# A hybrid decoder layer: the last residual addition leaves the vector engines and is done by accumulating stores

## The chip, the cores and the metric

The kernel runs on one core of a Trainium2 chip. The core has five engines that work side by side and meet through semaphores: TensorE (PE, with its weight loads shown as PEld), VectorE (DVE), ScalarE (ACT), GpSimd (POOL) and SyncE (SP). Sixteen DMA engines move data between the device memory (HBM) and the on-chip memory (SBUF). SP, ACT and POOL issue transfers; those of SP and ACT run on hardware queues, those of POOL on a software queue.

The metric is the device time of one execution in microseconds (us). It was 1841.93 us as the median of three runs (1841.57 to 1843.07).

## The reference

One inference step of a one-layer decoder trunk on 256 prompt tokens and 8 x 8 sample tokens, 320 tokens in all, with a model width of 2048. Cut to what bears on the change:

```python
def decoder_layer(x, ssm_state, ssm_conv_state, ffn_conv_state, p):
    h = rms_norm(x, p["norm_mix_pre"])
    proj = h @ p["w_in"]
    ...
    mix = jnp.concatenate([gate_out, ssm_out], axis=-1) @ p["w_out"]
    x = x + rms_norm(mix, p["norm_mix_post"])
    f, new_ffn_conv = conv_ffn(rms_norm(x, p["norm_ffn_pre"]), ffn_conv_state,
                               p["ffn_w_up"], p["ffn_conv_w"], p["ffn_conv_b"], p["ffn_w_down"])
    x = x + rms_norm(f, p["norm_ffn_post"])
    return x, new_ssm, new_ssm_conv, new_ffn_conv, chunk_v
```

The second-last `x` is called x1 in the kernel. The output y is x1 plus the normed FFN result f, and this last line is the one that the change rewrites. The norm is f times the reciprocal root of the mean of its squares over the width (one number for each token), times a weight for each column.

## The kernel before

Activations lie transposed: 128 partitions carry the columns of one of 16 column blocks (KD = 16), and the free dimension carries the 320 tokens (NT = 320). A tile such as `acc` is therefore 128 x 16 x 320 in single precision. The output `o_y` in HBM has the same layout, so that a store of two column blocks writes 128 rows of 2 x 320 numbers, 2560 bytes each.

Every matmul is done as three on TensorE: weights and activations are each split into a high and a low part, and high x high, high x low and low x high are summed (lines 128 to 130, in `accumulate`). Weights stream in as slabs of 512 KB (`slab`): SP loads a slab into one of three raw buffers (line 115), ScalarE makes the high part (line 117, three buffers), VectorE the low part (line 119, three buffers). The raw buffer is free for the next load once VectorE has read it.

The kernel runs in two halves. The first, the mixers, ends with x1 in `acc_mix` (line 962). The second, the FFN, has eleven groups g of 512 columns each. `ffn_up(g)` multiplies by the up-projection, applies the short convolution and the gate; `chunk_out(ffn_w_down, g, ...)` multiplies by the down-projection and adds the result to `acc_ffn` (line 210, VectorE). The loop runs one group ahead: `ffn_up(g + 1)` stands in the program before `chunk_out` of group g. Instructions are put in order by a list scheduler that goes by program order and by when they are ready.

In the last group `last(nb)` follows each column block: ScalarE squares it (line 258), GpSimd or, for the last two blocks, VectorE adds the squares up (line 259), and ScalarE multiplies the block by the norm's weight (line 1065). After the last block comes the tail. TensorE sums the squares over the columns (`token_sums`, line 241), VectorE forms the reciprocal root in eleven small operations (`rsqrt_of`, lines 224 to 230), and TensorE spreads it to all partitions (`spread`, line 248), where it stays in PSUM as `r4`. Then, for q from 0 to 7, two column blocks at a time:

```python
        for q in range(KD // n):
            ks = slice(n * q, n * q + n)
            f = acc[:, ks, :]
            dve.tensor_tensor(out=f, in0=f, in1=r4.unsqueeze(1).to_broadcast([P, n, NT]), op=ALU.mult)
            (dve if q in (2, 5, 7) else pool).tensor_tensor(out=f, in0=f, in1=x1[:, ks, :], op=ALU.add)
            (sp, act)[q % 2].dma_start(o_y[:, ks, :], f)
```

The multiplication is line 1084, the addition line 1085 (three on VectorE, five on GpSimd), the store line 1086 (four from SP, four from ACT). `o_y` isn't written anywhere else.

Of the kernel before, what the change touches and what calls it, by code (L numbers as in the profile page):

```python
# [9 lines left out]
F32 = mybir.dt.float32  # L10
# [3 lines left out]
ALU = mybir.AluOpType  # L14
# [3 lines left out]
P = 128  # L18
# [3 lines left out]
NT = NP + NS  # L22
D = 2048
KD = D // P
# [10 lines left out]
def hybrid_step(  # L35
# [10 lines left out]
    act, dve, pool, pe, sp = nc.scalar, nc.vector, nc.gpsimd, nc.tensor, nc.sync  # L46
# [10 lines left out]
    def misc(name):  # L57
        return ms.tile([P, 512], F32, tag="ms", name=name)
# [45 lines left out]
    def first():  # L104

        return tc.high_priority(offset=200000)
# [3 lines left out]
    def slab(src):  # L110
        n = src.shape[2]
        with tc.high_priority(offset=100000):
            m = n * src.shape[1]
            raw = wp.tile([P, 1024], F32, tag="wraw", name="wraw", bufs=3)
            slab_load.append(sp.dma_start(raw[:, :m].rearrange("p (a n) -> p a n", n=n), src).ins)
            hi = wp.tile([P, 1024], F32R, tag="whi", name="whi", bufs=3)
            act.copy(hi[:, :m], raw[:, :m])  # L117
            lo = wp.tile([P, 1024], F32R, tag="wlo", name="wlo", bufs=3)
            dve.tensor_tensor(out=lo[:, :m], in0=raw[:, :m], in1=hi[:, :m].bitcast(F32), op=ALU.subtract)  # L119

        def block(k, c):
            o = k * n + c * P
            return hi[:, o:o + P], lo[:, o:o + P]
        return block

    def accumulate(ps, w, xhi, xlo, first, last):
        whi, wlo = w
        pe.matmul(ps, whi, xhi, start=first, stop=False)  # L128
        pe.matmul(ps, whi, xlo, start=False, stop=False)  # L129
        return pe.matmul(ps, wlo, xhi, start=False, stop=last).ins  # L130

    def rows_of(w, k0, nk, c0, n):
        return w[k0 * P:(k0 + nk) * P, c0:c0 + n].rearrange("(k p) n -> p k n", p=P)
# [6 lines left out]
    def tick():  # L140
        while bg:
            try:
                next(bg[0])
                return
            except StopIteration:
                bg.pop(0)
# [51 lines left out]
    def chunk_out(w, ck, hi, lo, begins, done=None, rate=1):  # L198

        for nb in range(KD):  # L200
            if nb % 2 == 0:
                wb = slab(rows_of(w, 4 * ck, 4, P * nb, 256))
            ps = mm.tile([P, 512], F32, tag="mm", name=f"pd_{ck}_{nb}")
            for k in range(4):
                made = accumulate(ps[:, :NT], wb(k, nb % 2), hi[:, k, :], lo[:, k, :], k == 0, k == 3)
            with first():
                if begins:
                    act.copy(acc[:, nb, :], ps[:, :NT])
                else:
                    dve.tensor_tensor(out=acc[:, nb, :], in0=acc[:, nb, :], in1=ps[:, :NT], op=ALU.add)  # L210
            if done is not None:
                done(nb)
            if nb % 2 == 1:
                for _ in range(rate):
                    tick()
        pd_last.append(made)


    def rsqrt_of(ss, scale, n, rows=P):

        v = tp.tile([P, n], F32, tag=f"rs_v{n}", name="rs_v")[:rows]
        r = tp.tile([P, n], F32, tag=f"rs_r{n}", name="rs_r", bufs=3)[:rows]
        t = tp.tile([P, n], F32, tag=f"rs_t{n}", name="rs_t")[:rows]
        dve.tensor_scalar(out=v, in0=ss, scalar1=scale, scalar2=EPS, op0=ALU.mult, op1=ALU.add)
        dve.tensor_scalar(out=r.bitcast(I32), in0=v.bitcast(I32), scalar1=-0.5, scalar2=float(0x5F3759DF),
                          op0=ALU.mult, op1=ALU.add)
        for _ in range(3):
            dve.scalar_tensor_tensor(out=t, in0=v, scalar=-0.5, in1=r, op0=ALU.mult, op1=ALU.mult)
            dve.tensor_tensor(out=t, in0=t, in1=r, op=ALU.mult)
            ins = dve.scalar_tensor_tensor(out=r, in0=t, scalar=1.5, in1=r, op0=ALU.add, op1=ALU.mult).ins  # L230
        rsqrt_ins.append(ins)
        return r
# [3 lines left out]
    def token_sums(*sqs):  # L236

        ps = misc("tsum")
        for c, o in enumerate((0, P, NT - P)):
            for i, sq in enumerate(sqs):  # L240
                pe.matmul(ps[:, c:c + 1], sq[:, o:o + P], ones[:, 0:1], start=i == 0, stop=i == len(sqs) - 1)
        return ps[:, 0:3]

    def spread(r, out=None):

        ps = misc("spread")
        for c, o in ((2, NT - P), (0, 0), (1, P)):
            pe.transpose(ps[:, o:o + P], r[:, c:c + 1].to_broadcast([P, P]), ident)
        if out is not None:
            act.copy(out, ps[:, :NT])  # L250
        return ps[:, :NT]
# [69 lines left out]
    with ExitStack() as mctx:  # L321
        op = mctx.enter_context(tc.tile_pool(name="op", bufs=1))
# [305 lines left out]
        with tc.tile_pool(name="sd", bufs=1) as sd:  # L628
# [307 lines left out]
            with first():  # L936
# [4 lines left out]
                r = rsqrt_of(ps, 1.0 / D, 3)  # L941
# [35 lines left out]
    x1 = acc  # L977


    with tc.tile_pool(name="fp", bufs=1) as fp:  # L980
# [88 lines left out]
        for g in range(NG):  # L1069
            hi, lo = nxt  # L1070
            if g < NG - 1:
                nxt = ffn_up(g + 1)
            if g == 0:
                acc = fp.tile([P, KD, NT], F32, name="acc_ffn")
            chunk_out(ffn_w_down, g, hi, lo, g == 0, last if g == NG - 1 else None)

        act.dma_start(o_fconv_p, ptf)

        r4 = spread(rsqrt_of(token_sums(sq4), 1.0 / D, 3))
        n = 2  # L1080
        for q in range(KD // n):
            ks = slice(n * q, n * q + n)
            f = acc[:, ks, :]
            dve.tensor_tensor(out=f, in0=f, in1=r4.unsqueeze(1).to_broadcast([P, n, NT]), op=ALU.mult)
            (dve if q in (2, 5, 7) else pool).tensor_tensor(out=f, in0=f, in1=x1[:, ks, :], op=ALU.add)
            (sp, act)[q % 2].dma_start(o_y[:, ks, :], f)


_OUTS = [
# [81 lines left out]
```

## Time and profile before

| | |
|---|---|
| median of three runs | 1841.93 us |
| the profiled execution | 1841.51 us |
| its span, first to last instruction | 1839.8 us |
| mean granted TensorE clock | 0.988 |
| last matmul of the FFN starts | 1820.16 us |
| factor spread over the partitions, ends | 1825.95 us |
| last VectorE addition ends | 1836.23 us |
| data moved by DMA | 294.65 MB, of it 14.82 MB written to HBM |

How to read the rows: L1084 is line 1084 of the kernel. A row of groups gives the line, the engine, the operation, output<-input, and the shortest, median and longest duration in nanoseconds, then the first and last start in us. A row of the timeline or of the chain of waits begins with the start and the duration in us; in brackets stands how long the engine sat idle before, and what ended it. A "q" behind an engine's name means its queue of transfers. A row of queues gives packets, megabytes and the share of sixteen engines' time. "DMA to landing" is the time from the issue to the arrival of the last byte. A row of DMA tenths or GB/s cuts its window into 40 equal slices. A row of windows begins with the stretch in us; then come its sum, the busy time and count of PE, PEld, DVE, ACT and POOL, the granted clock, the DMA share and GB/s.

### The profile page before, as it was taken

The numbers are of one execution on the slowest core, as the hardware profiler recorded it, in microseconds if no ns is written. First come the engines' busy times: TensorE is split into PE (matmuls) and PEld (weight loads), VectorE is DVE, ScalarE is ACT, GpSimd is POOL, SyncE is SP. The second block draws the span as 40 slices with busy tenths as digits, with TensorE's granted clock in tenths as the row PEclk, the third lists the DMA queues.
The fourth block names the chain that finished last, engine by engine and source line by source line (L and its number), as shares of the span: only waits on it lengthen the run. The fifth ranks groups of instructions, "written<-read, shape, count | busy, mean of one in ns | idle before, by whom it ended". The sixth has DMA issues, their size and how long they took to land.

```text
span 1839.8 us, 31095 instructions
## 1 busy us (share of the span) xinstructions
PE 1790.7 (97%) x12185; PEld 1749.9 (95%) x12185; DVE 1188.5 (65%) x2050; ACT 786.2 (43%) x1077; POOL 305.2 (17%) x624
## 2 busy tenths in 40 slices
PE   8999999999999999999899999999999999999996
PEld 8999999999888889999799999999999999999995
DVE  4448854556986968676876475656465665756575
ACT  5442544334434545344454443333334343434334
POOL 1001210000331321103522020101011010201004
PEclk8999999999999999999899999999999999999998
DMA  8655654445566465555455545554545555455542
GB/s 265 178 141 172 167 149 148 149 147 158 178 184 207 138 205 159 170 161 188 152 163 156 153 150 151 155 152 150 152 150 152 150 152 150 153 150 155 153 154 92
DMA packets 222994, 294.65 MB, mean 160 GB/s; under 512 B 16736, under 2 KB 150464, under 8 KB 222656
## 3 DMA queue, kind: packets, MB, share of 16 engines
q1 hardware_dynamic: 210256, 269.72, 48.8%
q10 hardware_dynamic: 10448, 16.10, 2.4%
q0 software_dynamic: 2144, 6.85, 1.3%
q8 instruction: 96, 1.57, 0.4%
q14 instruction: 50, 0.41, 0.1%
HBM read 277.80 MB, written 14.82 MB: 159 GB/s over the span
## 4 chain that ended last, share of the span: by engine, by line
PE 82%; issue 6%; DVE 5%; DMA 4%; POOL 1%; ACT 1%; ACTq 0%; POOLq 0%; DVEq 0%; SPq 0%
PE ps L128 17%; PE ps L130 17%; PE ps L129 17%; PE pd L129 9%; PE pd L128 9%; PE pd L130 9%; DVE wlo L119 1%; DMA out_ssm_state_sample<-st 1%; PE y_ps L830 1%; DMA cs<-dacs_d 1%; DMA st<-in_state_ssm 1%; DMA wraw<-in_w_in 1%; POOL acc_mix L962 1%; PE yo_ps L737 1%; DMA lb<-in_gate_ln_b 1%
## 5 line engine op out<-in xcount | busy, mean ns | idle before, releaser
L119 DVE TENSOR_TENSOR wlo<-wraw,whi 128x1024 fp32r<-128x1024 f32 (+1 forms) x476 | 588.1, 1236 | 444.4 <-ACT whi L117 442.5
L117 ACT CAST whi<-wraw 128x1024 fp32r<-128x1024 f32 (+1 forms) x476 | 496.9, 1044 | 763.2 <-PE ps L129 446.1
L128 PE MATMUL ps<-h_hi,whi 128*128 128x320 f32 x2528 | 787.9, 312 | 10.0 <-ACT whi L117 5.3
L130 PE MATMUL ps<-h_hi,wlo 128*128 128x320 f32 x2528 | 784.4, 310 | 2.0 <-DVE wlo L119 2.0
L129 PE MATMUL ps<-h_lo,whi 128*128 128x320 f32 x2528 | 783.9, 310 | 0.0
L128 PEld LDWEIGHTS ps<-h_hi,whi 128*128 128x128 f32 x2528 | 477.2, 189 | 15.3 <-ACT whi L117 6.4
L130 PEld LDWEIGHTS ps<-h_hi,wlo 128*128 128x128 f32 x2528 | 477.0, 189 | 4.3 <-DVE wlo L119 3.3
L129 PEld LDWEIGHTS ps<-h_lo,whi 128*128 128x128 f32 x2528 | 477.1, 189 | 1.4 <-issue 0.9
L128 PE MATMUL pd<-fhi,whi 128*128 128x320 f32 x704 | 217.5, 309 | 0.0
L129 PE MATMUL pd<-flo,whi 128*128 128x320 f32 x704 | 217.5, 309 | 0.0
L130 PE MATMUL pd<-fhi,wlo 128*128 128x320 f32 x704 | 217.5, 309 | 0.0
L128 PE MATMUL pd<-ohi,whi 128*128 128x320 f32 x448 | 140.4, 313 | 0.0
L129 PE MATMUL pd<-olo,whi 128*128 128x320 f32 x448 | 139.1, 311 | 0.0
L130 PE MATMUL pd<-ohi,wlo 128*128 128x320 f32 x448 | 138.7, 310 | 0.0
L128 PEld LDWEIGHTS pd<-fhi,whi 128*128 128x128 f32 x704 | 132.2, 188 | 0.0
L129 PEld LDWEIGHTS pd<-flo,whi 128*128 128x128 f32 x704 | 132.2, 188 | 0.0
L130 PEld LDWEIGHTS pd<-fhi,wlo 128*128 128x128 f32 x704 | 132.2, 188 | 0.0
L1016 POOL COPY ptf<-pad 128x2 f32<-128x2 f32 x88 | 21.1, 240 | 597.8 <-DVE pad L1004 597.3
L210 DVE TENSOR_TENSOR acc_ffn<-acc_ffn,pd 128x320 f32<-128x320 f32 x160 | 77.5, 484 | 39.5 <-PE pd L130 38.0
L128 PEld LDWEIGHTS pd<-ohi,whi 128*128 128x128 f32 x448 | 84.1, 188 | 2.8 <-issue 2.2
L129 PEld LDWEIGHTS pd<-olo,whi 128*128 128x128 f32 x448 | 84.1, 188 | 1.6 <-issue 1.2
L130 PEld LDWEIGHTS pd<-ohi,wlo 128*128 128x128 f32 x448 | 84.1, 188 | 0.2 <-issue 0.2
(271 smaller groups left out, 1594.8 us busy)
## 6 DMA issues: line engine op xcount, KB each, us to landing
wraw<-in_ffn_w_up SPq DMA_DIRECT2D x176, 512.0 KB, 3.7
wraw<-in_w_in SPq DMA_DIRECT2D x144, 512.0 KB, 3.7
wraw<-in_ffn_w_down SPq DMA_DIRECT2D x88, 512.0 KB, 3.5
wraw<-in_w_out SPq DMA_DIRECT2D x64, 512.0 KB, 3.5
st<-in_state_ssm SPq DMA_DIRECT2D x40, 256.0 KB, 3.5
out_ssm_state_sample<-st ACTq DMA_DIRECT2D x32, 256.0 KB, 2.7
cs<-dacs_d SPq DMA_DIRECT2D x16, 320.0 KB, 4.2
xr<-in_xT SPq DMA_DIRECT2D x4, 640.0 KB, 4.3
```

Of the source, the lines that this page charges most:

```text
L117: act.copy(hi[:, :m], raw[:, :m])
L119: dve.tensor_tensor(out=lo[:, :m], in0=raw[:, :m], in1=hi[:, :m].bitcast(F32), op=ALU.subtract)
L128: pe.matmul(ps, whi, xhi, start=first, stop=False)
L129: pe.matmul(ps, whi, xlo, start=False, stop=False)
L130: return pe.matmul(ps, wlo, xhi, start=False, stop=last).ins
L210: dve.tensor_tensor(out=acc[:, nb, :], in0=acc[:, nb, :], in1=ps[:, :NT], op=ALU.add)
L737: pe.matmul(ps_yo[row:row + 32, :256], cms[:, b, :], st[:, 256 * r:256 * r + 256], start=b % 4 == 0, stop=b % 4 == 3, tile_position=(0, row))
L830: pe.matmul(ps[64 * i:64 * i + 64, cols], w(hl), x(hl, m, cpx), tile_position=(0, 64 * i), **flags)
L962: added.append((dve if kt < 2 else pool).tensor_tensor(out=a, in0=a, in1=xr[q][:, k, :], op=ALU.add).ins)
L1016: pool.tensor_copy(ptf[:, k, :], pad[:, 256:258])
```

## The change

x1 is stored to the output `o_y` whole, by one transfer on ACT's queue, at the second FFN group (g = 1), ahead of that group's `chunk_out`. In the tail the additions of x1 are gone. Each multiplied pair of column blocks is stored by GpSimd's queue with an accumulating transfer, which adds it to what `o_y` holds. The pair q = 7 comes first in the program and is multiplied by GpSimd. Since GpSimd reads its factor from SBUF, ScalarE copies `r4` from PSUM into a new tile `r4s`. The other seven pairs are multiplied by VectorE as before, in the order 0 to 6.

```diff
             if g == 0:
                 acc = fp.tile([P, KD, NT], F32, name="acc_ffn")
+            if g == 1:
+                act.dma_start(o_y, x1)
             chunk_out(ffn_w_down, g, hi, lo, g == 0, last if g == NG - 1 else None)
 
         act.dma_start(o_fconv_p, ptf)
 
+
         r4 = spread(rsqrt_of(token_sums(sq4), 1.0 / D, 3))
+        r4s = fp.tile([P, NT], F32, name="r4s")
+        act.copy(r4s, r4)
         n = 2
-        for q in range(KD // n):
+
+        for q in (KD // n - 1, *range(KD // n - 1)):
             ks = slice(n * q, n * q + n)
             f = acc[:, ks, :]
-            dve.tensor_tensor(out=f, in0=f, in1=r4.unsqueeze(1).to_broadcast([P, n, NT]), op=ALU.mult)
-            (dve if q in (2, 5, 7) else pool).tensor_tensor(out=f, in0=f, in1=x1[:, ks, :], op=ALU.add)
-            (sp, act)[q % 2].dma_start(o_y[:, ks, :], f)
+            on, r = (pool, r4s) if q == KD // n - 1 else (dve, r4)
+            on.tensor_tensor(out=f, in0=f, in1=r.unsqueeze(1).to_broadcast([P, n, NT]), op=ALU.mult)
+            pool.dma_start(o_y[:, ks, :], f, accum_op=ALU.add)
```

## The prediction

> **What bounds the kernel now.** I read the busy shares first, then the chain of waits over the last 24 us, then each engine's timeline and the DMA traffic after the last matmul.
>
> ```profile
> span 1839.8 us, 31095 instructions
> ...
> PE 1790.7 (97%) x12185; PEld 1749.9 (95%) x12185; DVE 1188.5 (65%) x2050; ACT 786.2 (43%) x1077; POOL 305.2 (17%) x624
> ```
>
> TensorE sets the pace nearly everywhere, and the change removes no matmul. So it can gain only where TensorE stands still, and what it adds earlier costs only if it makes TensorE wait. The standstill is the tail:
>
> ```profile
> 1820.16 0.16 PE pd L130
> ...
> 1825.03 0.92 PE spread L248 x3
> 1825.97 3.01 DVE acc_ffn L1084 x4
> 1828.98 1.60 DVE acc_ffn L1085
> 1830.58 2.19 DVE acc_ffn L1084 x3
> 1832.77 1.38 DVE acc_ffn L1085
> 1834.15 0.74 DVE acc_ffn L1084
> 1834.92 1.31 DVE acc_ffn L1085
> ```
>
> From 1825.97 to 1836.23 the chain is VectorE alone: eight multiplications (one each 0.74 to 0.75 us apart) and three additions; GpSimd's five additions run beside it. This is the stretch that the change attacks. What comes behind VectorE is the last store:
>
> ```profile
> L1086 SPq DMA_DIRECT2D out_y<-acc_ffn x4: 332/344/357, 1828.4 to 1835.6; - x4
> L1086 ACTq DMA_DIRECT2D out_y<-acc_ffn x4: 338/338/338, 1829.9 to 1836.3; - x4
> ...
> DMA to landing us min/median/max: 2.1/2.2/2.2
> ```
>
> The last store is issued at 1836.3 and lands 2.2 later, at 1838.5; 1.3 more pass to the end of the span. Now the traffic of these stores, the window 1826 to 1840 in 40 slices of 0.35 us:
>
> ```profile
> GB/s 0 0 0 0 0 0 0 0 0 227 417 293 0 146 395 432 388 439 73 161 402 373 0 73 432 395 432 388 154 88 424 402 424 402 132 0 0 0 0 0
> ...
> q10 hardware_dynamic: 576, 1.31, 23.5%
> q1 hardware_dynamic: 576, 1.31, 23.5%
> ```
>
> The reader is to see two things. The first slice with traffic is 1829.15 to 1829.5 and about half full, and the first store was issued at 1828.4: 0.7 to 1.0 us pass from an issue to data, and I use 1.0. The last slice with traffic ends at 1838.25, which is 1.55 before the end of the span. And the engines are already busy for 47% of 14 us, which is 6.6 us, at 400 GB/s and more whenever they move: eight stores cost 6.6 us of pure transfer even if they are all ready at once. VectorE's removed work therefore uncovers a transfer floor a few us behind it.
>
> **The change part by part.**
>
> VectorE: three additions go (1.60, 1.38 and 1.31 in the chain) and one multiplication (0.74). Seven are left: 1825.97 + 7 x 0.745 = 1831.2 instead of 1836.23. That is 5.0 us less on the present chain; the question is what ends later.
>
> GpSimd: five additions go. It gets the multiplication of the last two column blocks, ahead of everything else, and it can read the factor only from a copy in SBUF. The nearest rows:
>
> ```profile
> L250 ACT COPY r<-spread x2: 418/418/419, 52.4 to 937.4; 128x320 f32<-128x320 f32 x2
> L1085 POOL TENSOR_TENSOR acc_ffn<-acc_ffn,acc_mix x5: 1526/1542/2124, 1826.9 to 1833.4; 128x640 f32<-128x640 f32 x5
> ```
>
> The copy is the same operation as L250, 0.42 us, and ScalarE is idle there. GpSimd's multiplication has the shape of its additions, 1.54 us; the 2.12 fell to one that ran beside a VectorE addition, which no longer exists. The spread ends at 1825.95; with 0.05 for each of three handovers (the issue gap seen between engines in the chain): copy to 1826.42, multiplication to 1828.02, first accumulating store issued at 1828.07. The other seven stores stand behind this multiplication in GpSimd's queue, so the first of VectorE's results, ready at 1826.7, waits 1.9 us (its store comes second) where today it is handed on at once.
>
> Issue: eight stores leave SP and ACT (0.34 each, no one behind them) and go to GpSimd. Plain loads that GpSimd issues are the only price in the trace:
>
> ```profile
> L580 POOL DMA_DIRECT2D bs<-in_gate_b_s x4: 536/538/567, 56.4 to 404.1; - x4
> ...
> DMA to landing us min/median/max: 4.0/4.1/6.6
> ```
>
> ```profile
> L579 POOL DMA_DIRECT2D w<-in_gate_w x1: 532/532/532, 347.4 to 347.4; - x1
> ...
> DMA to landing us min/median/max: 1.8/1.8/1.8
> ```
>
> An issue takes 0.53 whether it carries 256 KB or 8 KB, so the eighth begins at 1828.07 + 7 x 0.53 = 1831.8, after VectorE's last result at 1831.2: the issues, not VectorE, come last before the transfers. The fixed part of a GpSimd transfer is 1.8 (8 KB, next to no data), that of the present stores 2.2 - 6.6/8 = 1.4. So I add 0.4 to the 1.0 above: data from 1828.07 + 1.4 = 1829.5. Bounds: 0.0 and 1.0 to add.
>
> Transfer: this is the term that no row shows. An accumulating store must fetch the old y beside f, so it moves 2.62 MB more on the read side. **Lower bound**: the second read hides completely, 6.6 us as today. **Upper bound**: each store waits for the one before it; 2.2 + 0.4 for the later start and 0.8 for its second read (6.2 below, over eight) make 3.4, times eight is 27 us. **Taken**: both reads one after the other through the same engines. What reading from HBM costs them at full load is in the traffic of the start, 5 to 25 us, where loads saturate the engines:
>
> ```profile
> DMA  9999999999999799999999999999999999999999
> GB/s 386 416 419 435 410 430 412 367 375 291 264 277 256 295 385 461 406 424 430 389 402 430 410 414 410 406 410 397 307 225 225 217 274 246 234 205 254 352 389 393
> ```
>
> At the 420 GB/s of its better slices 2.62 MB take 6.2 us; 6.6 + 6.2 = 12.8 us. I take it because the present stores leave the engines no spare rate (420 GB/s out, 420 in, each alone). The Trainium skill's page "Collectives: The Full Stack", section "The bandwidth ceiling: the fold count and why AG ≠ RS ≠ AR", says that a reduction in the DMA needs two source reads on the same read ring and measures it at half the rate of a copy (a ratio of 1.93). By that ratio the transfer would be an estimated 12.7 us and the span would end at 1843.75; by the plain store's row it ends at 1837.65. No run so far shows an accumulating transfer.
>
> Store of x1 during the FFN: one issue on ACT, about 0.36 (that of a 1 MB store, below), and 2.62 MB of traffic, 6.2 us at 420 GB/s, among the weight loads. x1 is final after its last addition:
>
> ```profile
> L962 POOL TENSOR_TENSOR acc_mix<-acc_mix,xr x14: 867/1131/1937, 885.7 to 910.3; 128x320 f32<-128x320 f32 x14
> ```
>
> That is before 913 us, and line 1068 to 1075 put the store behind two further up-projections, so nothing behind it on ACT's queue is held for data. Can it delay TensorE?
>
> ```profile
> 1034.06 3.89 SPq L115 DMA_DIRECT2D wraw<-in_ffn_w_up  x2
> ```
>
> ```profile
> 1035.24 1.05 ACT L117 CAST whi<-wraw 128x1024 fp32r<-128x1024 f32 x1 [2.15 <-PE ps L129]
> 1038.76 1.05 ACT L117 CAST whi<-wraw 128x1024 fp32r<-128x1024 f32 x1 [2.47 <-PE ps L129]
> 1042.28 1.05 ACT L117 CAST whi<-wraw 128x1024 fp32r<-128x1024 f32 x1 [2.47 <-PE ps L129]
> ```
>
> ```profile
> L115 SPq DMA_DIRECT2D wraw<-in_ffn_w_up x144: 367/368/379, 1016.6 to 1745.1; - x144
> ...
> DMA to landing us min/median/max: 3.3/3.6/5.1
> ```
>
> With three raw buffers, the load issued at 1034.06 feeds the third cast from there, at 1042.28; it lands after 3.6, so 4.6 us are spare, and behind the cast stand two more slabs of 3.52 us in converted form, less 2.3 for cast and subtraction: 4.7. Together 9.3 against 6.2 of delay if the store went wholly ahead. I cost it at nothing; uncovered, it would be 6.2. An earlier store of 1 MB on ACT's queue speaks for that:
>
> ```profile
> 181.00:187.00 6.00, 6.00 (x43) 6.00 (x42) 6.00 (x12) 2.45 (x3) 1.60 (x2) 1.00 0.90 299
> ```
>
> ```profile
> L565 ACTq DMA_DIRECT2D out_chunk_v_prompt<-vt x1: 362/362/362, 181.0 to 181.0; - x1
> ```
>
> TensorE (the first column behind the sum of 6.00) stays busy for 6.00 of 6.00 us with the engines' share at 0.90. The accumulating stores must wait for this store to land, which is some 800 us earlier.
>
> **Sum.** 1828.07 + 1.4 + 12.8 + 1.55 = 1843.8, against 1839.8: 4.0 us more. The profiled execution took 1841.51, 0.4 under the median of 1841.93; carried to that median the forecast is **1846.0 us**. The break-even is a transfer of 1839.8 - 1.55 - 1829.5 = 8.75 us, 1.33 times the plain one.
>
> **The rivals.**
>
> B, the second read hides. At the tail, read and write sides work at once, the y fetch costs the engines nothing, and each row takes what it takes now. Then 1829.5 + 6.6 + 1.55 = 1837.65: 2.2 less, **1839.8 us**. It decides below 1.33 times the plain transfer. For it: the engines idle in gaps of the present tail, and loads and stores run together at 181 us. Against it: 420 GB/s is reached in either direction alone. Even here the floor is the 6.6 us of bytes: without the added 0.4, 2.6 are gained, not VectorE's 5.0. Only if the scheduler put the first VectorE result's store ahead of GpSimd's multiplication could 1.3 more go.
>
> C, accumulating rows are much dearer, or one store waits for the last. Three times the plain row gives 19.8 us of transfer: 1850.9, 11 more, 1853 us. Wholly serial stores give 1828.07 + 27 + 1.3 = 1856.4, 16.6 more, **1858.5 us**. Against the serial form: today's second store is issued at 1829.9, before the first (1828.4 + 2.2) has landed, so stripes of y aren't held to overlap. For dear rows: nothing in the trace bounds them.
>
> D, the x1 store starves the weight loads: its rows are 20 KB, a load's 1 or 2 KB, and if engines alternate row by row the loads crawl for 6.2 us. The 9.3 us of cover speak against it; uncovered, with the forecast's tail, 1846.0 + 6.2 = **1852 us**. The Trainium skill, "DMA: Bandwidth & Descriptors", section "Queues, rings and completion order", says that an engine alternates between queues by whole packets; that is this rival's mechanism, and the trace above shows it with rows of 8 KB only, without a stall.
>
> E, the change does nothing where it matters: the floor falls at the old end, within 1 us of 1841.9.
>
> **How the numbers follow.** Forecast 0.55, B 0.20, C 0.16, D 0.05, E 0.04. A measurement of this kernel can tell about 0.2%, 3.7 us, from no change. The forecast's own range, from a start of 0.4 earlier or 0.6 later and a transfer of 11 to 14 us, is 1.8 to 5.8 more, 1843.7 to 1847.7; some six tenths of it lie above 3.7. Slower: 0.33 + 0.16 + 0.05 = 0.54. Faster by 3.7 needs B with the other order of GpSimd's queue: 0.04. Within: the rest, 0.42. The range runs from 1839.3, which takes in most of B, to 1853, which takes in D and the milder half of C; about 0.03 lie below it and 0.09 above.
>
> **What would show it.** In the changed profile: seven multiplications on VectorE ending near 1831.2; GpSimd's eight issues at 0.53 from 1828.07 to 1832.3; all traffic of the tail on the software queue, from about 1829.5, dense, and 12.8 us long. If it ends after 6.6 us, the taken price is wrong and B holds; if gaps stand between stores, C. TensorE in the second FFN group should show no new wait on a weight load, and the wraw landing may rise to 10 for two or three loads. The forecast falls if rows of the accumulating queue take under 1.3 times the present ones, or if the tail's start is moved by something upstream.

## The result and the profile after

| | before | after |
|---|---|---|
| median, six runs each | 1842.29 us | 1848.87 us |
| ratio, 95% interval | | 1.0034 [1.0023, 1.0046] |
| once more, 22 and 11 runs | 1841.21 us | 1847.48 us |
| ratio, 95% interval | | 1.0031 [1.0021, 1.0041] |
| span of the profiled execution | 1839.8 us | 1846.0 us |
| "tail": end of the spread to end of the span | 13.85 us | 22.1 us |

The change makes the kernel about 6 us slower; 4 were forecast, with 1.8 to 5.8 as the forecast's own range. I call the stretch from the end of the spread to the end of the span the tail. It is the measure for the profiles, since the work ahead of it starts some microseconds earlier or later from run to run.

First the chain of waits of the changed kernel behind the last matmuls (start, duration, what):

```profile
1823.04 0.92 PE spread L248 x3
...
1823.98 0.43 ACT r4s L1084
1824.41 0.07 issue
1824.48 1.55 POOL acc_ffn L1091
1826.03 0.30 issue
1826.33 6.26 POOL out_y L1092 x7
1832.59 0.89 POOLq L1173
```

VectorE has left the chain. Its own row, from the timeline, ends at 1829.64, 5.7 us after the spread, where it ended 10.3 after it before:

```profile
1824.43 5.21 DVE L1091 TENSOR_TENSOR acc_ffn<-acc_ffn,spread 128x640 f32<-128x640 f32 x7 [1.45 <-ACT r4s L1084]
```

So the change did what it set out to do on VectorE. The stores, by line and by queue (the window of the queue's row is 1826 to 1846):

```profile
L1092 POOL DMA_DIRECT2D out_y<-acc_ffn x8: 937/2092/3304, 1826.3 to 1830.2; - x8
L1076 ACTq DMA_DIRECT2D out_y<-acc_mix x1: 339/339/339, 910.7 to 910.7; - x1
...
DMA to landing us min/median/max: 4.8/9.7/13.7
```

```profile
DMA  0009387998899999999999999999999531000000
GB/s 0 0 0 82 41 113 143 210 169 123 159 179 169 195 200 179 184 210 205 200 215 195 215 195 215 195 220 205 205 210 220 102 61 20 10 0 0 0 0 0
...
q0 software_dynamic: 1152, 2.62, 77.4%
```

Three things are to be seen. The engines are full (nines), yet move some 200 GB/s where the plain stores moved 400 and more. Their busy time is 77.4% of 20 us, 15.5 us, where the plain stores needed 6.6. And the early store of x1 was issued at 910.7, long before the second FFN group: the list scheduler put it right behind x1's last addition, which starts at 908.7.

Finer windows give the ends of that traffic: 1826 to 1834 in slices of 0.2 us, and 1842 to 1846 in slices of 0.1.

```profile
GB/s 0 0 0 0 0 0 0 0 0 205 38 38 90 90 128 102 179 205 205 192 192 166 141 115 115 154 154 166 179 192 192 141 192 192 192 205 192 205 154 192
```

```profile
GB/s 77 51 102 0 77 0 77 0 26 0 26 0 26 0 0 0 0 0 0 0 0 0 0 0 0 0 0 0 0 0 0 0 0 0 0 0 0 0 0 0
```

Traffic begins between 1827.8 and 1828.0 and is thin for 1.2 us behind its first slice; it ends at about 1843.3, after a last 1.3 us in which only a few engines still work. Then 2.7 us pass to the end of the span.

### The profile page after: what moved, and what is told of

It reads as the page before. It is cut to its first block, busy times and chain, and to the rows that moved or that the text cites. A ratio compares the mean times of both kernels' runs of the same rounds, so it can differ in the third digit from the quotient of the medians.

```text
span 1846.0 us, 31083 instructions
## 1 busy us (share of the span) xinstructions
PE 1789.7 (97%) x12185; PEld 1747.7 (95%) x12185; DVE 1183.0 (64%) x2046; ACT 786.8 (43%) x1078; POOL 306.5 (17%) x628
## 4 chain that ended last, share of the span: by engine, by line
PE 84%; issue 6%; DVE 4%; DMA 4%; ACT 1%; POOL 1%; POOLq 0%; SPq 0%; ACTq 0%; DVEq 0%
PE ps L128 17%; PE ps L130 17%; PE ps L129 17%; PE pd L129 9%; PE pd L128 9%; PE pd L130 9%; DVE wlo L119 1%; PE y_ps L830 1%; DMA st<-in_state_ssm 1%; PE yo_ps L737 1%; DMA wraw<-in_w_in 1%; DMA cs<-dacs_d 1%; ACT whi L117 1%; DMA lb<-in_gate_ln_b 1%; PE sg L595 0%
## 5 line engine op out<-in xcount | busy, mean ns | idle before, releaser
L128 PEld LDWEIGHTS ps<-h_hi,whi 128*128 128x128 f32 x2528 | 476.1, 188 | 14.7 <-ACT whi L117 5.7
```

## The experiments

The two theories that had to be told apart first: the price of the tail is the second read of an accumulating store (T1), or the software queue, whose issues took 0.94 us and more instead of 0.53 (T2).

**Plain stores on GpSimd's queue.**

```diff
-            pool.dma_start(o_y[:, ks, :], f, accum_op=ALU.add)
+            pool.dma_start(o_y[:, ks, :], f)
```

> The changed kernel with its eight last stores still on GpSimd's queue but plain: y is f times its norm, x1 is overwritten (the last addition is left out). Theory T1 (the second read is the price): rows fall from 0.239 to 0.10 us, the transfer from 15.5 to about 6.6 us, and the tail from the end of the spread to the end of the span falls from 22.1 to 12.5-14 us; the time is 1.5 us below to 0.5 above the kernel before. Rival T2 (the software queue is slow, because GpSimd writes the descriptors: its issues took 0.9 to 3.3 us instead of 0.53): rows or the gaps between them stay, the transfer stays over 12 us, the tail stays over 19 us and the time 4 us or more above before.

Measured: ratio 0.9981 [0.9971, 0.9991]; span 1836.7, tail 12.9 us. The issues, and the queue's row in the window 1826 to 1836.7:

```profile
L1092 POOL DMA_DIRECT2D out_y<-acc_ffn x8: 539/539/585, 1826.1 to 1829.9; - x8
```

```profile
q0 software_dynamic: 640, 2.62, 61.1%
```

61.1% of 10.7 us is 6.5 us of transfer on the same queue: T1 holds against T2: the price belongs to accumulating and not to the queue. Whether the second read takes the time or the addition itself, no run separates. Even the long issues belong to the accumulation, since the plain ones take 0.54. The queue costs something else, seen in the window 1832.7 to 1836.7 (slices of 0.1 us), beside the kernel free_add below, which stores by SP and ACT, in the window 1830.3 to 1834.3:

```profile
GB/s 410 410 461 410 461 410 461 410 410 410 410 256 154 0 0 0 0 0 0 0 0 0 0 0 0 0 0 0 0 0 0 0 0 0 0 0 0 0 0 0
```

```profile
GB/s 461 410 410 410 410 410 410 410 410 410 410 435 410 410 384 410 435 410 410 410 410 461 256 26 0 0 0 0 0 0 0 0 0 0 0 0 0 0 0 0
```

Thirteen slices with traffic leave 2.7 us to the end of the span, twenty-four leave 1.6. The span ends 1.1 us later behind the software queue, whether the store is plain or accumulates. The other runs agree: 2.7 to 3.0 us where the last stores stand in the software queue, 1.6 to 1.7 where they stand in those of SP and ACT.

**GpSimd's multiplication undone**, and with it the copy of the factor.

```diff
-        for q in (KD // n - 1, *range(KD // n - 1)):
+        for q in range(KD // n):
...
-            on, r = (pool, r4s) if q == KD // n - 1 else (dve, r4)
-            on.tensor_tensor(out=f, in0=f, in1=r.unsqueeze(1).to_broadcast([P, n, NT]), op=ALU.mult)
+            dve.tensor_tensor(out=f, in0=f, in1=r4.unsqueeze(1).to_broadcast([P, n, NT]), op=ALU.mult)
```

> The changed kernel without GpSimd's multiplication: VectorE does all eight, in the order 0 to 7, no copy of the factor. T1 with the transfer as the bound: the first store is issued about 0.8 us after the spread instead of 2.4, so the tail shrinks by 1.5 us, from 22.1 to 20.6, and the time by about 1.5 us (ratio to before about 1.0026 instead of 1.0034). If the issues or VectorE set the end instead: VectorE's last result comes 0.7 us later and the tail is 22 to 23 us.

Measured: ratio 1.0030 [1.0018, 1.0041], tail 21.4 us (spread to 1829.40, span 1850.8). The first store is issued 1.15 us after the spread instead of 2.37, but the tail is only 0.65 shorter. Its traffic begins 2.6 us after the spread instead of 3.9, but the last 1.3 us of it move one row at a time (26 GB/s in every second slice of 0.1 us is a row of 2560 bytes; the window is 1846.8 to 1850.8), where the changed kernel has up to four:

```profile
GB/s 26 0 26 0 26 0 26 0 26 0 26 0 26 0 0 0 0 0 0 0 0 0 0 0 0 0 0 0 0 0 0 0 0 0 0 0 0 0 0 0
```

The difference to the changed kernel's ratio lies inside the intervals; the sign in the profile is as expected, the size under half of the 1.5 us. GpSimd's multiplication shows no gain; VectorE was not last.

**Fewer and larger, more and smaller accumulating stores**, both against dve_all:

```diff
-            pool.dma_start(o_y[:, ks, :], f, accum_op=ALU.add)
+            if q % 2:
+                k4 = slice(n * q - n, n * q + n)
+                pool.dma_start(o_y[:, k4, :], acc[:, k4, :], accum_op=ALU.add)
```

> As dve_all, but the accumulating stores are four of four column blocks each (rows of 5120 bytes) instead of eight of two. If the price goes by bytes (0.239 us per 2560), rows take 0.48, the transfer stays 15.3 us and starts 0.75 us later than in dve_all: tail about 21.3 us. If two reads cost 0.205 and each row or descriptor 0.034 more, rows take 0.445 and the transfer 14.2 us: tail about 20 us. If a cost per store weighs (issue up to 3.3 us), four fewer stores gain more than 2 us.

```diff
-            pool.dma_start(o_y[:, ks, :], f, accum_op=ALU.add)
+            for k in (n * q, n * q + 1):
+                pool.dma_start(o_y[:, k, :], acc[:, k, :], accum_op=ALU.add)
```

> As dve_all, with sixteen accumulating stores of one column block each (rows of 1280 bytes). The rows so far, 0.238 us for 2560 bytes and 0.434 for 5120, lie on 0.195 us per 2560 bytes (1.9 times the plain 0.102: two reads) plus 0.043 per row. Theory T1' (two reads plus a fixed cost per row): 0.14 us per row, transfer 128 x 0.14 = 18 us, tail about 23.5 us, 2 more than dve_all. Rival (the price goes by bytes alone, and the larger rows were quicker because there were fewer stores in flight): 0.119 per row, transfer 15.3, tail 21 to 22 us. Issues: 16 x 0.9 = 14.4 us if an issue costs by rows and not by bytes, just under the transfer.

Measured: four stores, ratio 1.0029 [1.0019, 1.0040], tail 19.4 us; sixteen stores, 1.0039 [1.0025, 1.0053], tail 21.9 us. The queue's rows, of rows_5k in 1826 to 1846 and of rows_1k in 1826 to 1848.6:

```profile
q0 software_dynamic: 576, 2.62, 69.9%
```

```profile
q0 software_dynamic: 2304, 2.62, 80.3%
```

Per engine and row (with its share of the semaphore packets) that is 0.142 us for 1280 bytes (80.3% of 22.6 over 128 rows), 0.242 for 2560 (77.4% of 20 over 64) and 0.437 for 5120 (69.9% of 20 over 32). The steps are 0.100 for 1280 bytes and 0.195 for 2560; a plain row of 2560 takes 0.102 (61.1% of 10.7 over 64). So a row costs 1.9 to 2.0 times the plain bytes, as two reads would, and about 0.04 us more at each of the three lengths. The Trainium skill, "Collectives: The Full Stack", section "The bandwidth ceiling: the fold count and why AG ≠ RS ≠ AR", has the factor, 1.93, for the reduction in a collective, and puts it down to two reads on one ring; the slope here agrees with it, while at this row length the whole row costs 2.4 times, which its factor alone doesn't give.

These are packet times, and the packets of one engine overlap: 18.1 us of them fit in about 16.4 us of traffic with sixteen stores, 14.0 in 13.4 with four. By the length of the traffic (15.5 us with eight stores) a row costs 0.128, 0.242 and 0.419 us, and the steps are 1.7 to 2.2 times the plain bytes. So about twice the plain rate holds either way; the fixed 0.04 us is a fit to packet times and less firm. The overlap is also why the tails follow in order only in part: with sixteen stores I expected 2 us more than dve_all and got 0.5.

**The accumulation aimed at SBUF.**

```diff
-            pool.dma_start(o_y[:, ks, :], f, accum_op=ALU.add)
+            pool.dma_start(x1[:, ks, :], f, accum_op=ALU.add)
```

> The changed kernel with its accumulating stores aimed at x1 in SBUF instead of y in HBM (y keeps x1 alone, so the last addition doesn't reach the output). If the price is the accumulation itself, two reads through one engine whatever the memory: rows 0.20 to 0.24 us, transfer 13 to 15.5 us. If it is the read of HBM at the tail (its delay or its rate): rows fall to 0.10 to 0.13 us and the transfer to 7 to 8 us.

In the one execution on record the span is 1842.3 and the tail 20.1 us. The queue in the window 1825 to 1843, slices of 0.45 us:

```profile
GB/s 0 0 159 199 188 182 165 199 210 182 194 188 199 176 205 188 199 199 188 199 199 216 199 205 194 233 193 199 211 216 199 120 23 0 0 0 0 0 0 0
...
q0 software_dynamic: 1152, 2.62, 80.0%
```

80.0% of 18 us over 64 rows is 0.225 us per row: without any HBM the price is nearly the same. What HBM adds is 0.017 per row or 1.1 us in all by packet time, and 1.9 us by the length of the traffic (1826.0 to 1839.6 here, 13.6 us, against 15.5). Part of it is seen at the start: here the traffic begins at its full 160 to 200 GB/s, in the changed kernel it stays at 38 to 128 GB/s for 1.2 us, and in dve_all at 26 to 166 for 1.4.

**The early store of x1 alone.**

```diff
             if g == 0:
                 acc = fp.tile([P, KD, NT], F32, name="acc_ffn")
+            if g == 1:
+                act.dma_start(o_y, x1)
             chunk_out(ffn_w_down, g, hi, lo, g == 0, last if g == NG - 1 else None)
```

> The kernel before with nothing but the early store of x1 to y added (the last stores overwrite it). The prediction's step (the cover of 9.3 us hides it): no change, within 1 us, tail 13.8 us, no new wait of TensorE. Rival D (it starves the weight loads): TensorE waits between 910 and 940 us, and the time rises by 2 to 6 us.

Measured: ratio 0.9994 [0.9984, 1.0004]; tail 13.8 us. The store was issued at 911.1. TensorE's waits from 880 to 1000 us, of before and then of x1_only (who for whom: sum, times, longest):

```profile
PE spread L248 <- DVE rs_r L230: 2.6, 1, 2.6
PE ps L128 <- ACT h_hi L302: 2.1, 1, 2.1
PE ps L130 <- DVE wlo L119: 1.2, 1, 1.2
PE ps L128 <- ACT whi L117: 0.3, 1, 0.3
```

```profile
PE ps L128 <- ACT h_hi L302: 2.1, 1, 2.1
PE ps L130 <- DVE wlo L119: 1.4, 3, 0.7
PE spread L248 <- DVE rs_r L230: 1.2, 1, 1.2
```

The loads themselves were held up to 9.5 us (median 4.5; 3.6 in the FFN before), close to the 3.6 + 6.2 that the prediction allowed for a store that goes wholly ahead. ScalarE's conversions felt it: between 900 and 960 us they waited for a slab five times, 7.2 us in all, where before it was once, 3.7 us. TensorE hardly did: its waits on a slab's low part (wlo) are three instead of one, 0.2 us more, and its waits in this window sum up to 4.7 us instead of 6.2. The cover held.

**What the change would be worth with the addition free**: plain stores from SP and ACT, VectorE multiplies all (the diff is against dve_all).

```diff
-            pool.dma_start(o_y[:, ks, :], f, accum_op=ALU.add)
+            (sp, act)[q % 2].dma_start(o_y[:, ks, :], f)
```

> What the change would be worth if the addition cost nothing: x1 to y early, VectorE multiplies all eight pairs, and plain stores from SP and ACT write f times its norm (the addition of x1 is left out). By the prediction's steps VectorE ends 6.0 us after the spread instead of 10.3, the stores follow, 1.0 to first data and 6.6 of transfer: tail 9.5 to 10.5 us instead of 13.8, the time 3.5 to 4.5 us under before (ratio 0.998). If the plain transfer bound it already, the tail would not fall below 12.

Measured: ratio 0.9985 [0.9974, 0.9996]; tail 9.8 us (spread to 1824.48, span 1834.3). With eight multiplications VectorE ends 4.3 us earlier after the spread than before the change, and 4.0 of them are a gain in the tail. The other 0.3 pass behind VectorE's last result, where the traffic now runs without gaps (the free_add row above).

**A version between both kernels**: the early store of x1, one accumulating store of the first four column blocks, additions for the rest (the diff is against the kernel before and leaves out the early store).

```diff
+            if q == 1:
+                pool.dma_start(o_y[:, :2 * n, :], acc[:, :2 * n, :], accum_op=ALU.add)
+            if q < 2:
+                continue
-            (dve if q in (2, 5, 7) else pool).tensor_tensor(out=f, in0=f, in1=x1[:, ks, :], op=ALU.add)
+            (dve if q in (4, 7) else pool).tensor_tensor(out=f, in0=f, in1=x1[:, ks, :], op=ALU.add)
```

> A version between both kernels: the first four column blocks go out by one accumulating store with rows of 5120 bytes (issued once VectorE has multiplied them), the other twelve by additions (two on VectorE, four on GpSimd) and plain stores as before. Transfer 8 x 0.434 + 48 x 0.102 = 8.4 us, hidden under VectorE's 8 x 0.745 + 2 x 1.4 = 8.8 us: tail 12.3 to 12.9 us instead of 13.8, the time about 1.2 us (0.07%) under before. If the plain stores wait behind the accumulating rows on each engine, or the software queue's later end counts, the gain is gone: tail 13.5 to 15 us.

Measured: ratio 1.0007 [0.9997, 1.0017]; tail 14.7 us. Neither reason that I had written for a miss was the main one: VectorE ended 11.1 us after the spread, since one of its additions, beside GpSimd's, took 3.63 us:

```profile
1828.41 3.63 DVE L1091 TENSOR_TENSOR acc_ffn<-acc_ffn,acc_mix 128x640 f32<-128x640 f32 x1
```

So the second form put VectorE's additions last (GpSimd takes q = 2, 3, 4, 5; VectorE adds 6 and 7 after its eight multiplications).

> As mix_5k, but VectorE multiplies all eight pairs before it adds the last two, so that its additions don't stand among GpSimd's first ones (in mix_5k one of them took 3.63 us). Theory (VectorE's wait for GpSimd ate the gain): VectorE ends 9.0 to 9.6 us after the spread instead of 11.1, tail 12.5 to 13.1 us against 13.8 before, the time 0.7 to 1.3 us (0.05%) under before, which five rounds hardly tell from nothing. Rival (the accumulating rows hold up the plain stores): tail stays at 14 us or more.

Measured: ratio 0.9997 [0.9988, 1.0006]; tail 14.3 us. The additions of mix_late by line:

```profile
L1092 POOL TENSOR_TENSOR acc_ffn<-acc_ffn,acc_mix x4: 1853/1869/1883, 1832.0 to 1836.5; 128x640 f32<-128x640 f32 x4
L1092 DVE TENSOR_TENSOR acc_ffn<-acc_ffn,acc_mix x2: 814/2239/3664, 1835.4 to 1839.0; 128x640 f32<-128x640 f32 x2
```

A VectorE addition of the same shape takes 3.66 us beside GpSimd's and 0.81 after them. VectorE still ends 10.3 us after the spread, as before the change. The theory for mix_late had the cause right and its cure wrong: moving the additions only moved the wait. A tail over 14 us was also the rival's sign (accumulating rows that hold up the plain stores). The profile leaves it a small part at most: VectorE ends as late as before the change, and only 0.4 us more than before pass behind it, in which the software queue moves nothing any more. No version that computes everything is measurably faster than the kernel before.

**The changed kernel once more.**

> The changed kernel once more, for its tail and its ratio with more runs. If the tail alone makes the difference, as the two profiles say (22.1 against 13.8 us, with the body unchanged), the ratio is 1.0045 and not 1.0034; the first measurement's interval of 1.0023 to 1.0046 just holds it. If the early store of x1 or the other order of the FFN gives something back, the ratio stays at 1.0034 or lower while the tail stays at 22 us.

Measured: ratio 1.0031 [1.0021, 1.0041], tail 22.4 us. The tail alone, 8.5 us more, would be 1.0046; the measured ratio is about 2.8 us short of it, so something ahead of the tail seems to give time back. The store of x1 alone points the same way, by 1.1 us, but its interval includes no difference at all. The two kernels' instruction orders part only near 910 us, and between the first residual product (line 961) and the FFN's factor (line 250) the changed kernel takes 54.8 us in both profiles, x1_only 54.9, where before took 55.5. From the first residual product to the end of the spread it is 943.7 and 943.3 us in the changed kernel's two profiles, 944.1 before. So the profiles show 0.4 to 0.7 us of the 2.8. The rest isn't explained and may be chance: by the same sum plain_pool came out 2.5 us quicker than its tail says, and free_add 1.3 us slower.

## Why the prediction came out as it did

The direction and its cause were right. The time of 1848.9 lies inside the wide range of 1839.3 to 1853, which was to take in most of the rivals, but 1.2 us above the forecast's own range of 1843.7 to 1847.7: the tail's price was sized at half, and the transfer, its largest term, lies above the 11 to 14 us that were allowed. The terms, each from the profile of after:

| step | predicted | measured |
|---|---|---|
| spread to first issue | 2.12 | 2.37 |
| issue to first traffic | 1.4 | 1.5 to 1.7 |
| transfer | 12.8 | about 15.4 |
| last traffic to end of span | 1.55 | 2.7 |
| tail | 17.9 | 22.1 |

- VectorE's seven multiplications end 5.7 us after the spread; 5.25 was said. The first of them waited for ScalarE's copy of the same PSUM tile (the bracket in its row), which the prediction took to run beside it. That they no longer set the end was right.
- **Transfer**: "both reads one after the other" was right in kind; a row's price rises at about twice the plain rate, and the SBUF form shows that it isn't mainly HBM's. Mis-sized by 2.6 us: the second read was taken at the 420 GB/s of loads, 6.2 us, with nothing for the row itself and nothing for its start. By packet times a fixed 0.04 us per row makes up the 2.6 (64 rows for each engine). By the length of the traffic, the stores to SBUF lasted 13.6 us, 0.8 over the forecast, and 1.9 came only with HBM. How the 2.6 divide between the two stays open. Rival B, the hidden read, falls with it: break-even was 1.33 times the plain transfer, measured is 2.3.
- **Issue**: 0.53 was taken from plain loads and holds for plain stores (0.54), not for accumulating ones: eight took 7.15 us. That is hidden, as the transfer is longer.
- **End**: 1.55 was carried over from SP's and ACT's stores; behind the software queue it is 2.7, a term that was treated as fixed though the change moved the queue. The prediction asked what stands behind GpSimd's multiplication in its instruction queue, and not what stands at the end of its transfer queue.
- **GpSimd's multiplication** delays the first store: 2.37 against 1.15 us after the spread, where 2.12 was worked out; undone, it gives the tail 0.65 and not 1.2.
- **Store of x1**: costed at nothing, and no change was measured (0.9994 [0.9984, 1.0004]). Where it stands was wrong: I followed the program's g = 1, the scheduler issued it at 910.7.
- Rival C in its milder form has part of the truth, rows dearer than two reads; wholly serial stores don't occur. Rival D falls with x1_only (the prediction's rows at 181 us show that no stall came there, not how an engine alternates between queues); rival E falls with the tail.
- The sum's miss of 4.2 us in the tail was partly made good ahead of it, by about 2 us in the medians, of which the profiles show 0.4 to 0.7. No step foresaw that: it is luck that the time of 1848.9 lies nearer the forecast of 1846.0 than the tail does.

## What to carry to other kernels

An addition moved into an accumulating store isn't removed: here the transfer engines took 2.3 times the plain transfer for it, so ask first whether the stores already fill the end of the kernel. Five microseconds of vector work were traded for 9 of transfer; such a trade can pay only where the transfer is hidden. When a store changes queue, count what the new queue does at the end of the kernel as well as at the start.

## What the runs showed of the hardware

- A plain store through the software queue was as fast as through the hardware queues (6.5 against 6.6 us for 2.62 MB), and its rows of 2560 bytes seem to have gone out two to a packet: 640 packets, of them 128 under 512 bytes, so 512 for 1024 rows, where the hardware queues had 1152. The accumulating stores had 1152.
- An accumulating issue on GpSimd doesn't cost by bytes: 0.85 to 0.94 us at the least for 128 rows of 1280, 2560 and 5120 bytes alike (no run has another number of rows). When eight stand in line they overlap and each looks longer, up to 3.3 us; the eight still end 7.15 us after the first began.
- The kernel's end comes 2.7 to 3.0 us after the last traffic of the software queue and 1.6 to 1.7 us after that of the hardware queues.
- A VectorE addition with both inputs in SBUF was held up beside GpSimd's additions: 3.66 us against 0.81. The Trainium skill, "SBUF — State Buffer", section "Who interferes with whom", says that such an instruction contends with a GpSimd instruction that reads SBUF; mix_late's two additions agree, in one row. In the kernel before, VectorE's three additions beside GpSimd's took 1.31 to 1.60 us, also more than 0.81, so two adding engines gave it less than twice one.
